# Recurrence products regrouped and the scores' positive part moved to ScalarE, in a hybrid attention and RWKV-7 step

## The chip, the core and the metric

The kernel runs on one core of a Trainium2 chip. The metric is the device time of one execution in microseconds. TensorE does the matrix products, VectorE, ScalarE and GpSimd the elementwise work, and SyncE issues nearly all transfers. Each engine works through its own queue in order.

## The reference

One layer over 2048 prompt tokens and 8 x 8 sample tokens, with a model width of 1024. A combined projection feeds two groups of eight heads of 64: stick-breaking attention, and an RWKV-7 recurrence with a matrix state per head. Both outputs are gated and concatenated, projected back, added to the input and normalised.

```python
# attention: z are the scaled scores plus a bias per head
log_keep = where(mask, log_sigmoid(-z), 0.0)
between = cumsum(log_keep, reverse=True) - log_keep
a = where(mask, exp(log_sigmoid(z) + between), 0.0)
out = einsum('bhqk,bkhd->bqhd', a, v)

# recurrence, per head, for every token
sa = einsum('bhvk,bhk->bhv', S, a_t)
S = S * w_t + sa[..., None] * b_t + v_t[..., None] * k_t
y = einsum('bhvk,bhk->bhv', S, r_t)
```

## The kernel before

The program is planned as a list of operations, each with an engine, a cost, the data it reads and writes, and a priority. `Plan.issue` walks this list like a simulator of its own and emits the operations in the order in which they would start; so the costs, the limits on PSUM banks per kind (`LIMITS`), the latency put on a transfer and the priorities set the order of every engine's queue. All instructions pass through one wrapper and carry line 63 in the profile; they are told apart by the names of their tiles.

The prompt is cut in four slabs of 512 tokens (`hf`), and each slab's head columns in four groups of 128 (`j`), that is two heads. Per slab the projections (`project`, tiles `xh`, `xl`, `wp`; each float32 product is made of three reduced ones) have the lowest priority on TensorE and fill what the rest leaves. `attend(t, j)` handles 512 queries of two heads against all key blocks. Per 128 queries and head it makes a block: scores of 512 keys into a bank (`kt`, `qt`), `softmax_chain`, transposes of the result (`ident`, `T`), an Exp, and the product with the values (`At`, `vt`). In `softmax_chain` ScalarE takes |z + bias| into T, then Exp and Ln in place, VectorE takes max(z + bias, 0) into D, then a backward scan over T and D, and the last step subtracts. The score bank (kind `ZB`, two of them) is held until that last step.

`rw_unit(hf, j)` handles the recurrence of one slab and column group, in 8 chunks of 64 tokens. `rw_pairs` makes the products of keys and queries within a chunk, two heads of 64 rows each (`un.BK`, `un.AR`): for each half of the chunks first the four of head 0 into a bank of kind `EB`, then the four of head 1 into another, then a masked copy into `un.L`. `inverse_a` and `inverse_b` invert the triangular part, with a loop of 31 steps on VectorE. `seq` then does one chunk at a time, and its products on TensorE are called in this text by the names of the functions in the code:

- `fx` (rows named `VV,L`): `un.L` against the stacked state and values, head by head onto the two halves of the partitions
- `fu` (`XT,NN`): the inverse applied to the copy XT of that, one product per head, each into a bank of its own
- `fs` (`VV,BKT`): the new state, both heads on the lower half of the partitions, in different columns
- `fy` (`L,VV`, `AR,VV`, `RS,VV`): the output, two products of 128 rows and two of 64 rows

GpSimd prepares the decayed old state `sw`, and VectorE adds it to the result of `fs` and writes the next state. At the end, sample attention and the output projection (`woh`, `wol`, `orw`) share TensorE with the last attention blocks.

Of the kernel before, what the change touches and what calls it, by code (L numbers as in the profile page):

```python
# [9 lines left out]
F32 = mybir.dt.float32  # L10
# [69 lines left out]
class Plan:  # L80
# [90 lines left out]
    def issue(self, tables):  # L171
# [51 lines left out]
        while done < len(ops):  # L223
            best = None
            for e in engines:
                s, got = pick(e, free[e])
                if s < INF and (best is None or s < best[0]):
                    best = (s, e, got)
            s, e, got = best
            if got is None:  # L230
                got = pick(e, s)[1]
                if got is None:
                    continue
            avail[e].remove(got)
# [36 lines left out]
            done += 1  # L271
            free[e] = s + cost
            busy[e] += cost
            end = s + cost
            if o.lat:
                dma_free = max(dma_free, end + 650.0) + o.lat
                end = dma_free + 1200.0
            for j in outs[i]:
                lag = 0.0 if o.lat else self.LAG.get((e, ops[j].eng), 0.0 if ops[j].eng == e else 170.0)
                ready[j] = max(ready[j], end + lag)  # L280
                left[j] -= 1
                if not left[j]:
                    heapq.heappush(waiting[ops[j].eng], (ready[j], j))
# [59 lines left out]
class Kern:  # L343
# [522 lines left out]
    def rwkv_tiles(self, S):  # L866
# [4 lines left out]
        for i in range(2):  # L871
            u = Unit()
            u.id = i
            u.AR = S.tile([128, 8, 128], F32, "AR").t
            u.BK = S.tile([128, 8, 128], F32, "BK").t
            u.L = [S.tile([128, 8, 128], F32, f"L{h}").t for h in range(2)]
            u.NN = S.tile([128, 8, 64], F32, "NN").t
            nc.gpsimd.memset(u.NN, 0.0)
            u.RS = S.tile([64, 8, 64], F32, "RS").t
            u.WC = S.tile([64, 2, 8], F32, "WC").t  # L880
            self.units.append(u)

# [11 lines left out]
        self.XT = S.ring(2, [128, 64], F32, "XT")  # L894
        self.xts = S.tile([128, 64], F32, "xts")
        self.SW = S.ring(2, [64, 2, 64], F32, "SW")
# [54 lines left out]
    def rw_elem(self, hf, j, t0, N, c0, un):  # L951
# [52 lines left out]
        if smp:  # L1004
            self.copy(self.wc8.t, W3[:, :, 8], r=w3k, w=[self.wc8.k])
        else:
            for h in range(2):
                self.copy(un.WC[:, h, :], W3[self.HR[h], :, 64], r=w3k, w=[("WC", U, i) for i in range(8)])

        self.act(rn, zk, AF.Square, r=kk_, w=[rnk], scale=self.vec("k_k", j))  # L1010
        b3 = self.sums("EB", rn, rnk, self.scratch(hf, 0) if "3" in self.BO and not smp else None)
# [41 lines left out]
    def rw_pairs(self, un):  # L1053

        nc, U = self.nc, un.id
        for c4 in range(0, 8, 4):
            for h in range(2):
                bk = self.bank("EB")
                hr = self.HR[h]
                for i in range(4):  # L1060
                    def f(c=c4 + i, i=i, bk=bk, hr=hr):
                        self.mm(bk.t[:, 128 * i:128 * i + 128], un.BK[hr, c, :], un.AR[hr, c, :], True, True)
                    self.pe(222, f, r=[("AR", U, c4 + i), ("BK", U, c4 + i)], w=[bk.k], mode="C")
                self.tt(un.L[h][:, c4:c4 + 4, :], bk.t.rearrange("p (c x) -> p c x", x=128),
                        self.mask.rearrange("p (o x) -> p o x", o=1).to_broadcast([128, 4, 128]), ALU.mult,
                        r=[bk.k], w=[("L", U, h, c4 + i) for i in range(4)])
# [40 lines left out]
    def inverse_b(self, un):  # L1107
# [27 lines left out]
        self.dma(un.RS, un.AR[64:128, :, 64:128], r=ark, w=[("RS", U)], nbytes=131072)  # L1135

    def seq(self, hf, j, c, un):
        nc, U = self.nc, un.id
# [21 lines left out]
                self.act(VV[lo, 0, 0], self.SP[:, j], AF.Copy, r=[("SP", j)], w=[ks])  # L1160
        lks = [("L", U, 0, c), ("L", U, 1, c)]
        nks = [("NN", U, h, b) for h in range(2) for b in range(2)]
        sw = self.SW.next()
        wc = un.WC[:, :, c:c + 1]
        self.pool(450, lambda: nc.gpsimd.tensor_tensor(out=sw.t, in0=VV[lo, s_, 0], in1=wc.to_broadcast([64, 2, 64]), op=ALU.mult), r=[ks, ("WC", U, c)], w=[sw.k])
# [5 lines left out]
        xt = self.XT.next()  # L1171
        self.copy(xt.t, bx.t[:, 0:64], r=[bx.k], w=[xt.k], prio=-0.5)
        bu = [self.bank("XB"), self.bank("XB")]
        for h in range(2):
            def fu(h=h):
                self.mm(bu[h].t[lo, 0:64], un.NN[hr[h], c, :], xt.t[hr[h], :], True, True)
            self.pe(107, fu, r=nks + [xt.k], w=[bu[h].k], prio=-0.5, mode="B")
        self.copy(VV[lo, s_, 1, 0, :], bu[0].t[lo, 0:64], r=[bu[0].k], w=[ku + (0,)], prio=-0.5)
        self.act(VV[lo, s_, 1, 1, :], bu[1].t[lo, 0:64], AF.Copy, r=[bu[1].k], w=[ku + (1,)], ps=True, prio=-0.5)
        kus = [ku + (0,), ku + (1,)]  # L1180
        bs = self.bank("XB")
        def fs():
# [12 lines left out]
        def fy():  # L1195
            for h in range(2):
                self.mm(yb.t[hr[h], y0:y0 + 64], VV[:, s_, 1, h, :], un.L[h][:, c, 64:128], True, False)
            for h in range(2):
                rt = un.RS[:, c, :] if h else un.AR[lo, c, 64:128]
                self.mm(yb.t[hr[h], y0:y0 + 64], VV[lo, s_, 0, h, :], rt, False, True)  # L1200
        self.pe(500, fy, r=kus + [kv, ks, ("AR", U, c), ("RS", U)] + lks, w=[yb.k], mode="A")
# [363 lines left out]
    def softmax_chain(self, zb, n, bias, bk, car, first, last, rings):  # L1565
# [275 lines left out]
```

## Time and profile before

| | |
|---|---|
| median of three runs | 2165.12 us (2162.68 to 2172.65) |
| profiled execution | 2174.32 us, its span 2172.6 us |
| mean granted TensorE clock | 0.965 of full speed |
| busy: TensorE, weight loads, VectorE, ScalarE, GpSimd | 2068.2, 1570.7, 1764.3, 1322.7, 252.9 us |
| transfers | 380.88 MB, 175 GB/s on average |

The page gives busy time and the chain of waits for the whole span. A float32 product appears as two records, and matmul records overlap: one's end is modelled and lies past the start of the next, so starts are compared and not durations.

### The profile page before, as it was taken

What the parts mean: (1) busy time and instruction counts of PE and PEld (TensorE: products, weight loads), DVE (VectorE), ACT (ScalarE), POOL (GpSimd) and SP (SyncE); (2) the same over time, 40 slices, a digit from 0 to 9 for tenths busy, and PEclk for the clock granted to TensorE, in tenths of its full rate; (3) what the DMA queues carried; (4) which work ended last, traced back from release to release, by engine and by line L of the source; (5) the groups of instructions that cost most, each with busy time, mean ns of one, the idle gap of its engine ahead of it and who ended that gap; (6) DMA issues with size and microseconds to landing.
All of it is one profiled execution on the core that took longest, in us unless ns stands there. A gap on an engine that the chain in (4) does not pass through costs nothing.

```text
span 2172.6 us, 43597 instructions
## 1 busy us (share of the span) xinstructions
PE 2068.2 (95%) x15386; PEld 1570.7 (72%) x15386; DVE 1764.3 (81%) x4085; ACT 1322.7 (61%) x2655; POOL 252.9 (12%) x594
## 2 busy tenths in 40 slices
PE   6799999979999999999999999999999899999998
PEld 6687887757776777777767777877776676767665
DVE  7797687664888889989899898898889798988842
ACT  6544453554655758677567486566468686867731
POOL 4221211100000201010011011011010100000000
PEclk9999989989999999999999999999999799999999
DMA  7975644637666385755634843755744757575654
GB/s 240 328 256 165 200 151 143 197 118 215 180 183 188 101 254 133 216 148 158 187 93 138 241 108 112 209 137 137 203 142 127 207 163 211 161 196 155 192 175 146
DMA packets 346551, 380.88 MB, mean 175 GB/s; under 512 B 127922, under 2 KB 247272, under 8 KB 346332
## 3 DMA queue, kind: packets, MB, share of 16 engines
q1 hardware_dynamic: 345948, 378.00, 59.8%
q8 instruction: 121, 1.98, 0.4%
q14 instruction: 98, 0.80, 0.1%
q0 software_dynamic: 384, 0.10, 0.0%
HBM read 268.94 MB, written 102.76 MB: 171 GB/s over the span
## 4 chain that ended last, share of the span: by engine, by line
PE 66%; DMA 6%; DVE 4%; ACT 2%; SPq 1%; issue 1%; POOL 0%; DVEq 0%; POOLq 0%; ACTq 0%
PE bank L63 66%; DVE D L63 2%; SPq L63 1%; DMA IMP<-d_im 1%; DMA IA<-d_ia 1%; ACT T L63 1%; DMA wp<-d_w 1%; DVE IMP L63 1%; DMA D<-d_g 1%; DVE T L63 0%; DMA d_o<-D 0%; DMA xs<-d_x 0%; DMA kt<-d_k 0%; DMA ev<-d_x 0%; DVE SPT L63 0%
## 5 line engine op out<-in xcount | busy, mean ns | idle before, releaser
L63 PE MATMUL bank<-xh,wp 128*128 128x512 f32 (+2 forms) x2704 | 798.5, 369 | 9.2 <-ACT wp L63 5.6
L63 PEld LDWEIGHTS bank<-xh,wp 128*128 128x128 f32 x2704 | 485.6, 194 | 83.9 <-ACT wp L63 7.4
L63 PE MATMUL bank<-xl,wp 128*128 128x512 f32 (+2 forms) x1352 | 495.5, 367 | 0.0
L63 ACT ACTIVATE T<-T 128x512 f32<-128x512 f32 (+3 forms) x608 | 340.9, 565 | 11.8
L63 PEld LDWEIGHTS bank<-xl,wp 128*128 128x128 f32 x1352 | 261.9, 194 | 33.4 <-issue 2.9
L63 ACT ACTIVATE At<-bank 128x512 f32<-128x512 f32 (+3 forms) x304 | 161.3, 530 | 197.2 <-PE bank L63 186.9
L63 DVE TENSOR_SCALAR D<-bank,sbb 128x512 f32<-128x512 f32 (+3 forms) x304 | 200.6, 661 | 54.6 <-ACT T L63 46.6
L63 DVE TENSOR_TENSOR_SCAN D<-T,car,D 128x512 f32<-128x512 f32 x180 | 230.9, 1283 | 14.5 <-ACT T L63 12.7
L63 PE MATMUL bank<-kt,qt 128*128 128x512 f32 (+3 forms) x640 | 216.7, 414 | 3.8 <-issue 3.3
L63 ACT ACTIVATE T<-bank,sbb 128x512 f32<-128x512 f32 (+3 forms) x304 | 187.7, 620 | 48.0 <-PE bank L63 36.3
L63 DVE SCALAR_TENSOR_TENSOR T<-bank,sbb,D 128x512 f32<-128x512 f32 (+3 forms) x304 | 200.6, 660 | 2.1 <-PE bank L63 0.4
L63 PE MATMUL bank<-woh,orw 128*128 128x512 f32 (+1 forms) x544 | 188.9, 411 | 3.8 <-ACT woh L63 2.8
L63 PE MATMUL bank<-ident,T 128*128 128x128 f32 (+1 forms) x1156 | 175.3, 275 | 13.1 <-DVE T L63 8.8
L63 DVE TENSOR_TENSOR IMP<-IMP,IA 128x2 f32<-128x2 f32 (+30 forms) x496 | 168.0, 339 | 22.3 <-POOL IA L63 16.3
L63 PEld LDWEIGHTS bank<-ident,T 128*128 128x128 f32 (+1 forms) x1156 | 129.3, 142 | 53.8 <-DVE T L63 16.0
L63 PE MATMUL bank<-At,vt 128*64 128x128 f32 x1992 | 149.0, 288 | 0.1
L63 PEld LDWEIGHTS bank<-At,vt 128*64 128x64 f32 x1992 | 111.9, 141 | 36.6 <-issue 28.7
L63 POOL COPY car<-D 128x1 f32<-128x1 f32 x180 | 48.9, 272 | 690.5 <-DVE D L63 639.1
L63 PEld LDWEIGHTS bank<-woh,orw 128*128 128x128 f32 (+1 forms) x544 | 99.5, 187 | 36.9 <-issue 11.9
L63 DVE TENSOR_REDUCE IMP<-IMP 128x1 f32<-128x2 f32 (+30 forms) x496 | 120.9, 244 | 4.9
L63 PEld LDWEIGHTS bank<-kt,qt 128*128 128x128 f32 x640 | 103.8, 196 | 14.3 <-issue 7.7
L63 POOL TENSOR_TENSOR SW<-VV,WC 64x128 f32<-64x128 f32 x128 | 67.8, 533 | 388.9 <-DVE VV L63 292.4
(325 smaller groups left out, 3449.3 us busy)
## 6 DMA issues: line engine op xcount, KB each, us to landing
wp<-d_w SPq DMA_DIRECT2D x198, 512.0 KB
d_w<-wp SPq DMA_DIRECT2D x66, 512.0 KB
kt<-d_k SPq DMA_DIRECT2D x80, 256.0 KB
wraw<-in_w_in SPq DMA_DIRECT2D x66, 256.0 KB
qt<-d_q SPq DMA_DIRECT2D x128, 128.0 KB
orw<-d_o SPq DMA_DIRECT2D x64, 256.0 KB
vt<-out_v_prompt SPq DMA_DIRECT2D x38, 256.0 KB
IA<-d_ia SPq DMA_DIRECT2D x64, 128.0 KB
```

The source lines that it names most:

```text
L63: return f(*[x.real() if isinstance(x, Lz) else x for x in a], **{k: x.real() if isinstance(x, Lz) else x for k, x in kw.items()})
```

## The change

There are six edits. (1) `rw_pairs` takes two banks at once and issues the products of head 0 and head 1 in turn; the plan is told half the cost for each. The limit of `EB` banks goes from 2 to 3. (2) `fu` is one product: XT has a column block per head with zeros in the other head's rows, so one 128-row product gives both heads side by side. The copy into XT is split, the lower half on VectorE, the upper on ScalarE. (3) `fs` writes head 0 to the lower and head 1 to the upper half of the partitions; `WN` holds the decays on 128 partitions for it, and GpSimd writes `sw` in two halves. (4) `fy` uses 128 rows everywhere: head 0 reads the state from a copy `sz` whose upper half is zero, head 1 multiplies with `RS` whose upper half is zero. (5) In `softmax_chain` the positive part is an activation. (6) The plan assumes that a transfer's data arrive 300 ns later than before.

```diff
-                end = dma_free + 1200.0
+                end = dma_free + 1500.0
...
-    LIMITS = {"PB": 3, "EB": 2, "MB": 1, ...
+    LIMITS = {"PB": 3, "EB": 3, "MB": 1, ...
...
-            for h in range(2):
-                bk = self.bank("EB")
-                hr = self.HR[h]
-                for i in range(4):
+            bks = [self.bank("EB") for _ in range(2)]
+            for i in range(4):
+                for bk, hr in zip(bks, self.HR):
...
-                    self.pe(222, f, r=[("AR", U, c4 + i), ("BK", U, c4 + i)], w=[bk.k], mode="C")
+                    self.pe(112, f, r=[("AR", U, c4 + i), ("BK", U, c4 + i)], w=[bk.k], mode="C", share=1.0)
...
-        sw = self.SW.next()
-        wc = un.WC[:, :, c:c + 1]
-        self.pool(450, lambda: nc.gpsimd.tensor_tensor(out=sw.t, in0=VV[lo, s_, 0], in1=wc.to_broadcast([64, 2, 64]), op=ALU.mult), ...)
+        sw, sz = self.SW.next(), self.SZ.next()
+        for h in range(2):
+            wc = un.WC[:, h, c:c + 1].to_broadcast([64, 64])
+            self.pool(250, lambda h=h, wc=wc: nc.gpsimd.tensor_tensor(out=sw.t[hr[h]], in0=VV[lo, s_, 0, h], in1=wc, op=ALU.mult), ...)
+        self.pool(170, lambda: nc.gpsimd.tensor_copy(sz.t[lo], VV[lo, s_, 0, 0]), r=[ks], w=[sz.k])
...
-        self.copy(xt.t, bx.t[:, 0:64], r=[bx.k], w=[xt.k], prio=-0.5)
-        bu = [self.bank("XB"), self.bank("XB")]
-        for h in range(2):
-            def fu(h=h):
-                self.mm(bu[h].t[lo, 0:64], un.NN[hr[h], c, :], xt.t[hr[h], :], True, True)
-            self.pe(107, fu, r=nks + [xt.k], w=[bu[h].k], prio=-0.5, mode="B")
+        self.copy(xt.t[lo, 0], bx.t[lo, 0:64], r=[bx.k], w=[(xt.k, 0)], prio=-0.5)
+        self.act(xt.t[hi, 1], bx.t[hi, 0:64], AF.Copy, r=[bx.k], w=[(xt.k, 1)], ps=True, prio=-0.5)
+        bu = self.bank("XB")
+        self.pe(224, lambda: self.mm(bu.t[lo, 0:128], un.NN[:, c, :], xt.t.rearrange("p h x -> p (h x)"), True, True), ...)
...
-                self.mm(bs.t[lo, 64 * h:64 * h + 64], BKT[:, s_, h, :], VV[:, s_, 1, h, :], True, True)
-        self.pe(270, fs, ...)
+                self.mm(bs.t[hr[h], 0:64], BKT[:, s_, h, :], VV[:, s_, 1, h, :], True, True)
+        self.pe(215, fs, ...)
...
-                rt = un.RS[:, c, :] if h else un.AR[lo, c, 64:128]
-                self.mm(yb.t[hr[h], y0:y0 + 64], VV[lo, s_, 0, h, :], rt, False, True)
-        self.pe(500, fy, ...)
+                st, rt = (VV[:, s_, 0, 1, :], un.RS[:, c, :]) if h else (sz.t, un.AR[:, c, 64:128])
+                self.mm(yb.t[hr[h], y0:y0 + 64], st, rt, False, True)
+        self.pe(330, fy, ...)
...
-        self.ts(d, z, bias, ALU.add, 0.0, ALU.max, r=[zb.k] + bk, w=[D.k])
+        self.act(d, z, AF.Relu, r=[zb.k] + bk, w=[D.k], bias=bias, ps=True)
```

Three places in the order of the queues show what moves. The first is TensorE at one `rw_pairs` of the second slab (`AR`, `BK` are the pair products, `bor` a sum within heads, `zL` the next unit's decay). Before:

```order
L63 MATMUL bank_4_67<-xh_183,bor_161 128x512
L63 MATMUL bank_1_64<-AR_87,BK_88 128x128 x4
L63 MATMUL bank_4_67<-xl_184,bor_161 128x512
L63 MATMUL bank_6_69<-xh_183,wp_190 128x512
L63 MATMUL bank_6_69<-xl_184,wp_190 128x512
L63 MATMUL bank_5_68<-ident_80,T_141 128x128 x4
L63 MATMUL bank_7_70<-kt_136,qt_138 128x512
L63 MATMUL bank_2_65<-AR_87,BK_88 128x128 x4
L63 MATMUL bank_1_64<-AR_87,BK_88 128x128 x4
```

In the change, at the same place:

```order
L63 MATMUL bank_2_65<-AR_87,BK_88 128x128
L63 MATMUL bank_4_67<-AR_87,BK_88 128x128
L63 MATMUL bank_2_65<-AR_87,BK_88 128x128
L63 MATMUL bank_7_70<-xl_192,bor_169 128x512
L63 MATMUL bank_4_67<-AR_87,BK_88 128x128
L63 MATMUL bank_5_68<-xh_191,wp_198 128x512
L63 MATMUL bank_1_64<-ident_80,T_149 128x128 x4
L63 MATMUL bank_6_69<-AR_87,BK_88 128x128 x4
L63 MATMUL bank_2_65<-AR_87,BK_88 128x128 x4
```

The first set of eight now changes bank at every product; the second set still comes as four and four.

The second place is TensorE at the end of a chunk step, from `fu` to `fy`. Before:

```order
L63 MATMUL bank_4_67<-XT_110,NN_99 64x64
L63 MATMUL bank_8_71<-XT_110,NN_99 64x64
L63 MATMUL bank_2_65<-xh_183,wp_190 128x512 x2
L63 MATMUL bank_2_65<-xl_184,wp_190 128x512
L63 MATMUL bank_7_70<-VV_107,BKT_106 64x64 x2
L63 MATMUL bank_1_64<-L_22_97,VV_107 64x64
L63 MATMUL bank_1_64<-L_23_98,VV_107 64x64
L63 MATMUL bank_1_64<-AR_95,VV_107 64x64
L63 MATMUL bank_1_64<-RS_101,VV_107 64x64
```

In the change the same groups (`fs` and `fy` of one step, and `fu` of the next):

```order
L63 MATMUL bank_8_71<-VV_111,BKT_110 64x64 x2
L63 MATMUL bank_6_69<-L_23_99,VV_111 64x64
L63 MATMUL bank_6_69<-L_24_100,VV_111 64x64
L63 MATMUL bank_6_69<-AR_97,SZ_117 64x64
L63 MATMUL bank_6_69<-RS_103,VV_111 64x64
...
L63 MATMUL bank_4_67<-XT_114,NN_101 64x128
```

`fs` and `fy` still stand together; `fu` is one row, twice as wide.

The third place is ScalarE in the last stage, where attention blocks follow each other. Before:

```order
L63 ACTIVATE T_141<-bank_7_70,sbb_159 128x512
L63 ACTIVATE T_141<-T_141 128x512 x2
L63 ACTIVATE At_145<-bank_4_67 128x512
L63 ACTIVATE T_140<-bank_6_69,sbb_159 128x512
L63 ACTIVATE T_140<-T_140 128x512 x2
```

In the change:

```order
L63 ACTIVATE T_149<-bank_4_67,sbb_167 128x512
L63 ACTIVATE D_151<-bank_4_67,sbb_167 128x512
L63 ACTIVATE T_149<-T_149 128x512 x2
L63 ACTIVATE At_152<-bank_1_64 128x512
L63 ACTIVATE T_148<-bank_6_69,sbb_167 128x512
L63 ACTIVATE D_150<-bank_6_69,sbb_167 128x512
```

The row that writes D stands between the Abs and the Exp of its block.

## Rows read from the trace of the kernel before

**Rows 1.** The page: busy time of the engines, and the chain of waits.
```profile
PE 2068.2 (95%) x15386; PEld 1570.7 (72%) x15386; DVE 1764.3 (81%) x4085; ACT 1322.7 (61%) x2655; POOL 252.9 (12%) x594
...
PE 66%; DMA 6%; DVE 4%; ACT 2%; SPq 1%; issue 1%; POOL 0%; DVEq 0%; POOLq 0%; ACTq 0%
```

**Rows 2.** Waits of TensorE by releaser: us in total, times, longest us.
```profile
PE bank L63 <- DVE L L63: 10.9, 2, 9.1
...
PE bank L63 <- DVE tmpke L63: 0.2, 1, 0.2
```

**Rows 3.** Stages: us, busy of PE, PEld, DVE, ACT, POOL, clock, DMA share, GB/s.
```profile
800.00:1000.00 200.00, 199.15 (x1549) 152.64 (x1548) 181.88 (x393) 151.14 (x297) 22.27 (x63) 1.00 0.61 169
1800.00:2000.00 200.00, 198.69 (x1460) 137.38 (x1460) 168.72 (x260) 143.95 (x280) 13.18 (x43) 1.00 0.65 187
```

**Rows 4.** Stage, instructions that read the score bias alone: busy of DVE, ACT, POOL.
```profile
1800.00:2000.00 200.00, 73.02 (x110) 34.70 (x55) 0.00 (x0) 1.00 0.65 187
```

**Rows 5.** Timeline of TensorE around two chunk steps: start us, us, instruction, count.
```profile
1098.97 0.34 PE L63 MATMUL bank<-VV,L 128*64 128x64 f32 x4
1099.23 0.50 PE L63 MATMUL bank<-xh,wp 128*128 128x512 f32 x1
...
1102.09 0.39 PE L63 MATMUL bank<-VV,BKT 128*64 128x64 f32 x3
...
1102.85 0.23 PE L63 MATMUL bank<-neg,idb 128*128 128x128 bf16 x1
...
1109.64 0.40 PE L63 MATMUL bank<-xh,wp 128*128 128x512 f32 x1
1109.97 0.33 PE L63 MATMUL bank<-XT,NN 64*64 64x64 f32 x4
1110.23 0.50 PE L63 MATMUL bank<-xh,wp 128*128 128x512 f32 x1
1110.57 0.39 PE L63 MATMUL bank<-xl,wp 128*128 128x512 f32 x1
1110.80 0.40 PE L63 MATMUL bank<-xh,wp 128*128 128x512 f32 x1
```

**Rows 6.** Timeline of TensorE at pair products: two units.
```profile
1037.05 1.16 PE L63 MATMUL bank<-AR,BK 64*128 64x128 f32 x8
1038.14 0.51 PE L63 MATMUL bank<-xh,wp 128*128 128x512 f32 x1
1038.57 1.71 PE L63 MATMUL bank<-AR,BK 64*128 64x128 f32 x16
...
1156.02 0.48 PE L63 MATMUL bank<-AR,BK 64*128 64x128 f32 x2
```

**Rows 7.** Groups of instructions by shape: busy us, mean ns, idle before.
```profile
L63 DVE TENSOR_SCALAR D<-bank,sbb 128x512 f32<-128x512 f32 x210 | 155.7, 743 | 20.3 <-ACT T L63 18.7 <-ACT rs L63 0.5
L63 ACT ACTIVATE T<-bank,sbb 128x512 f32<-128x512 f32 x210 | 143.6, 686 | 28.3 <-PE bank L63 26.2 <-DVE T L63 0.8
L63 POOL TENSOR_TENSOR SW<-VV,WC 64x128 f32<-64x128 f32 x128 | 67.8, 533 | 388.9 <-DVE VV L63 292.4 <-ACT tmpWi L63 56.2 <-DVE IMP L63 22.2
L63 ACT ACTIVATE VV<-bank 64x64 f32<-64x64 f32 x128 | 27.1, 212 | 44.8 <-PE bank L63 39.3 <-DVE tmprn L63 4.6
```

**Rows 8.** Timeline of ScalarE at one block of the last stage.
```profile
1886.33 0.68 ACT L63 ACTIVATE T<-bank,sbb 128x512 f32<-128x512 f32 x1
1887.04 1.29 ACT L63 ACTIVATE T<-T 128x512 f32<-128x512 f32 x2
1889.58 0.60 ACT L63 ACTIVATE At<-bank 128x512 f32<-128x512 f32 x1 [1.25 <-PE bank L63]
```

**Rows 9.** Timeline of VectorE at the same block.
```profile
1887.86 0.75 DVE L63 TENSOR_SCALAR D<-bank,sbb 128x512 f32<-128x512 f32 x1
1888.71 1.28 DVE L63 TENSOR_TENSOR_SCAN D<-T,car,D 128x512 f32<-128x512 f32 x1
1890.50 0.74 DVE L63 SCALAR_TENSOR_TENSOR T<-bank,sbb,D 128x512 f32<-128x512 f32 x1
```

More of the change, by code (lines that the diff above doesn't have):

```diff
@@ L375 @@
     NEV = 3
-    LIMITS = {"PB": 3, "EB": 2, "MB": 1, "SB": 1, "XB": 2, "YB": 1, "X": 2, "ZB": 2, "TB": 1, "OB": 1, "SA": 1, "SB2": 1, "OY": 4, "SM": 1, "YS": 1}
+    LIMITS = {"PB": 3, "EB": 3, "MB": 1, "SB": 1, "XB": 2, "YB": 1, "X": 2, "ZB": 2, "TB": 1, "OB": 1, "SA": 1, "SB2": 1, "OY": 4, "SM": 1, "YS": 1}
     def __init__(self, tc, I, O):
@@ L878, in rwkv_tiles @@
             nc.gpsimd.memset(u.NN, 0.0)
-            u.RS = S.tile([64, 8, 64], F32, "RS").t
+            u.RS = S.tile([128, 8, 64], F32, "RS").t
+            nc.gpsimd.memset(u.RS[64:128], 0.0)
+            u.WN = S.tile([128, 8], F32, "WN").t
             u.WC = S.tile([64, 2, 8], F32, "WC").t
@@ L893, in rwkv_tiles @@
         self.W3 = S.tile([128, 520], F32, "W3")
-        self.XT = S.ring(2, [128, 64], F32, "XT")
+        self.XT = S.tile([128, 2, 64], F32, "XT")
+        nc.vector.memset(self.XT.t, 0.0)
+        self.SZ = S.ring(2, [128, 64], F32, "SZ")
+        for x in self.SZ.slots:
+            nc.gpsimd.memset(x.t[64:128], 0.0)
         self.xts = S.tile([128, 64], F32, "xts")
-        self.SW = S.ring(2, [64, 2, 64], F32, "SW")
+        self.SW = S.ring(2, [128, 64], F32, "SW")
         self.IA = S.tile([128, 32, 32], F32, "IA")
@@ L1008, in rw_elem @@
                 self.copy(un.WC[:, h, :], W3[self.HR[h], :, 64], r=w3k, w=[("WC", U, i) for i in range(8)])
+            self.copy(un.WN, W3[:, :, 64], r=w3k, w=[("WN", U)])
         self.act(rn, zk, AF.Square, r=kk_, w=[rnk], scale=self.vec("k_k", j))
@@ L1056, in rw_pairs @@
         for c4 in range(0, 8, 4):
-            for h in range(2):
-                bk = self.bank("EB")
-                hr = self.HR[h]
-                for i in range(4):
+            bks = [self.bank("EB") for _ in range(2)]
+            for i in range(4):
+                for bk, hr in zip(bks, self.HR):
                     def f(c=c4 + i, i=i, bk=bk, hr=hr):
                         self.mm(bk.t[:, 128 * i:128 * i + 128], un.BK[hr, c, :], un.AR[hr, c, :], True, True)
-                    self.pe(222, f, r=[("AR", U, c4 + i), ("BK", U, c4 + i)], w=[bk.k], mode="C")
+                    self.pe(112, f, r=[("AR", U, c4 + i), ("BK", U, c4 + i)], w=[bk.k], mode="C", share=1.0)
+            for h, bk in enumerate(bks):
                 self.tt(un.L[h][:, c4:c4 + 4, :], bk.t.rearrange("p (c x) -> p c x", x=128),
@@ L1134, in inverse_b @@
             self.dma(un.L[h][0:64, :, 0:64], un.AR[self.HR[h], :, 0:64], r=ark, w=[("L", U, h, c) for c in range(8)], nbytes=131072)
-        self.dma(un.RS, un.AR[64:128, :, 64:128], r=ark, w=[("RS", U)], nbytes=131072)
+        self.dma(un.RS[0:64], un.AR[64:128, :, 64:128], r=ark, w=[("RS", U)], nbytes=131072)
     def seq(self, hf, j, c, un):
@@ L1162, in seq @@
         nks = [("NN", U, h, b) for h in range(2) for b in range(2)]
-        sw = self.SW.next()
-        wc = un.WC[:, :, c:c + 1]
-        self.pool(450, lambda: nc.gpsimd.tensor_tensor(out=sw.t, in0=VV[lo, s_, 0], in1=wc.to_broadcast([64, 2, 64]), op=ALU.mult), r=[ks, ("WC", U, c)], w=[sw.k])
+        sw, sz = self.SW.next(), self.SZ.next()
+        for h in range(2):
+            wc = un.WC[:, h, c:c + 1].to_broadcast([64, 64])
+            self.pool(250, lambda h=h, wc=wc: nc.gpsimd.tensor_tensor(out=sw.t[hr[h]], in0=VV[lo, s_, 0, h], in1=wc, op=ALU.mult), r=[ks, ("WC", U, c)], w=[(sw.k, h)])
+        self.pool(170, lambda: nc.gpsimd.tensor_copy(sz.t[lo], VV[lo, s_, 0, 0]), r=[ks], w=[sz.k])
         bx = self.bank("XB")
@@ L1170, in seq @@
         self.pe(215, fx, r=lks + [ks, kv], w=[bx.k], prio=-0.5, mode="A")
-        xt = self.XT.next()
-        self.copy(xt.t, bx.t[:, 0:64], r=[bx.k], w=[xt.k], prio=-0.5)
-        bu = [self.bank("XB"), self.bank("XB")]
-        for h in range(2):
-            def fu(h=h):
-                self.mm(bu[h].t[lo, 0:64], un.NN[hr[h], c, :], xt.t[hr[h], :], True, True)
-            self.pe(107, fu, r=nks + [xt.k], w=[bu[h].k], prio=-0.5, mode="B")
-        self.copy(VV[lo, s_, 1, 0, :], bu[0].t[lo, 0:64], r=[bu[0].k], w=[ku + (0,)], prio=-0.5)
-        self.act(VV[lo, s_, 1, 1, :], bu[1].t[lo, 0:64], AF.Copy, r=[bu[1].k], w=[ku + (1,)], ps=True, prio=-0.5)
+        xt = self.XT
+        self.copy(xt.t[lo, 0], bx.t[lo, 0:64], r=[bx.k], w=[(xt.k, 0)], prio=-0.5)
+        self.act(xt.t[hi, 1], bx.t[hi, 0:64], AF.Copy, r=[bx.k], w=[(xt.k, 1)], ps=True, prio=-0.5)
+        bu = self.bank("XB")
+        self.pe(224, lambda: self.mm(bu.t[lo, 0:128], un.NN[:, c, :], xt.t.rearrange("p h x -> p (h x)"), True, True), r=nks + [(xt.k, 0), (xt.k, 1)], w=[bu.k], prio=-0.5, mode="A")
+        self.copy(VV[lo, s_, 1, 0, :], bu.t[lo, 0:64], r=[bu.k], w=[ku + (0,)], prio=-0.5)
+        self.act(VV[lo, s_, 1, 1, :], bu.t[lo, 64:128], AF.Copy, r=[bu.k], w=[ku + (1,)], ps=True, prio=-0.5)
         kus = [ku + (0,), ku + (1,)]
@@ L1183, in fs @@
             for h in range(2):
-                self.mm(bs.t[lo, 64 * h:64 * h + 64], BKT[:, s_, h, :], VV[:, s_, 1, h, :], True, True)
-        self.pe(270, fs, r=[kb, kv] + kus, w=[bs.k], prio=-0.5, mode="A")
+                self.mm(bs.t[hr[h], 0:64], BKT[:, s_, h, :], VV[:, s_, 1, h, :], True, True)
+        self.pe(215, fs, r=[kb, kv] + kus, w=[bs.k], prio=-0.5, mode="A")
         last = c == 7
@@ L1188, in seq @@
             out = self.SP[:, j, h] if last else VV[lo, sn, 0, h, :]
-            self.stt(out, bs.t[lo, 64 * h:64 * h + 64], un.WC[:, h, c:c + 1], sw.t[:, h], ALU.mult, ALU.add,
-                     r=[bs.k, sw.k, ("WC", U, c)], w=[("SP", j)] if last else [("VVS", sn)], prio=-0.5)
+            self.stt(out, bs.t[hr[h], 0:64], un.WN[hr[h], c:c + 1], sw.t[hr[h]], ALU.mult, ALU.add,
+                     r=[bs.k, (sw.k, h), ("WN", U)], w=[("SP", j)] if last else [("VVS", sn)], prio=-0.5)
         if c == 0:
@@ L1198, in fy @@
             for h in range(2):
[L1199 to L1201 removed]
+                st, rt = (VV[:, s_, 0, 1, :], un.RS[:, c, :]) if h else (sz.t, un.AR[:, c, 64:128])
+                self.mm(yb.t[hr[h], y0:y0 + 64], st, rt, False, True)
+        self.pe(330, fy, r=kus + [kv, ks, sz.k, ("AR", U, c), ("RS", U)] + lks, w=[yb.k], mode="A")
     def rw_out(self, hf, j, t0, N, c0, un, yb):
```

## Prediction

> **What bounds the kernel now.** I read the page first: TensorE is busy 2068.2 us of a span of 2172.6 (95%), VectorE 81%, ScalarE 61%, GpSimd 12%, and the chain of waits is 66% TensorE, with nothing else above 6% [rows 1]. So TensorE's queue of work is the bound. What the change is worth is what it takes out of that queue, plus or minus what happens to the 104 us in which TensorE stood still. The list of TensorE's waits splits that idle time: 18 of its rows end on VectorE and sum to 58 us (the longest and the shortest are shown) [rows 2]. The stage table has VectorE at 181.9 of 200 us in the stretch from 800 to 1000, where TensorE is at 199.2, and ScalarE at 144 to 151 [rows 3]: ScalarE has room, VectorE nearly none.
>
> What a small product costs is not its duration, since matmuls overlap. It is the distance from its start to the next start, plus what its neighbours lose. Two 512-column products in a row start 0.23 us apart (1110.57 to 1110.80); the one before a small group takes 0.33 (1109.64 to 1109.97), the one after it 0.34 (1110.23 to 1110.57) [rows 5]. Each visit to a small group thus costs 0.21 us on top of the group itself.
>
> **The change, part by part.** There are 16 units of work (4 slabs of 512 tokens by 4 column groups), so 128 chunk steps, and each step has four small groups on TensorE.
>
> (a) *New state and output* (`fs`, `fy`). Today they stand together and take from 1102.09 to 1102.85, 0.76 us for 12 records [rows 5]: the two heads of `fs` write the same half of the columns and run one after the other, and the last four records of `fy` use 64 rows where the ones ahead use 128. In the change every group has its two heads on different column halves, and all use 128 rows. `fx` has that form today: 4 records, both heads at once, 0.26 us (1098.97 to 1099.23). The two halves of `fy` add four more steps. A step of 128 columns costs (1.16 - 0.48)/6 = 0.113 us, by the rows of eight and of two records of such a product [rows 6]; one of 64 columns costs half, 0.057. The sum is 0.26 + 4 x 0.057 = 0.49, and 0.27 x 128 = 34.6 us are saved. The rows of zeros that fill the operands up to 128 cost nothing: the estimate is made from `fx`, which has 128 rows. Bounds: 34.6, and 0 if the pairs did not overlap.
>
> (b) *`fu`* becomes one product of 128 columns instead of two of 64. Today the two run at once when they stand together (x4 at 1109.97, next start 0.26 later) [rows 5]; the order has them together in 110 steps and apart in 18, where I charge each the same 0.26. With the visits that is (110 + 36) x 0.47 = 68.6 us. The new form, two records of 128 columns, is not in the trace. Bounds: 0.26, as if the width cost nothing, and 0.41, a visit of two records with the same moving width (0.48 less the 0.07 by which a group outlasts the next start) [rows 6]. I take 0.41, the row nearest in width: 128 x (0.41 + 0.21) = 79.4. This part **loses** 11 us; at 0.26 it would win 8.
>
> (c) *Pair products* (`rw_pairs`), 256 of them in 32 sets of eight. Eight records of one head take 1.09 us to the next start; sixteen, where both heads stand together, 1.71 in all or 1.64, and not 2.18 [rows 6]. So heads on different row halves already overlap where they meet. A typical unit today is 8, 16 and 8 records in three visits: 3.82 + 0.63 = 4.45 us. With the heads alternating a set should take the 1.09 of one head, 1.30 with its visit. In the new order 18 of 32 sets are mostly alternated; the others still come head by head, because the second bank comes late. Ten units with one alternated set cost 1.30 + 2.60 (two visits of one head each) and save 0.55 each; three with two such sets save 1.85 each; two in between about 1.2 each; one with none loses 0.75. That is 12.7, taken as 13 us. Bounds: 0 (no more overlap than now) and 16 x 1.85 = 30.
>
> (d) *Relu on ScalarE.* It removes the VectorE pass that writes D, 320 of them, 743 ns for 512 columns. ScalarE's own pass of the same shape, bank and bias, the Abs, takes 686 ns [rows 7]. So at most 320 x 0.69 = 220 us go to ScalarE for about as much from VectorE, and none of it is TensorE's. Where it lands: in 1800 to 2000 ScalarE is busy 143.95 us [rows 3] with 55 Abs passes [rows 4]; 55 x 0.69 = 38 more makes 182 of 200. It fits, narrowly. One block shows the path: Exp and Ln ended at 1888.34 [rows 8], but the scan started at 1888.71, after the VectorE pass of 1887.86 to 1888.61 [rows 9]. With Relu ahead of Exp, Ln would end near 1889.0, so the scan is late by 0.3 and not by 0.69. The block holds its score bank from 1886.33 to 1891.24, 4.91 us; with two banks one block per 2.5 us is possible, and 55 in 200 us are one per 3.6. Cost on the path: zero, with that slack as the cover; without cover, 0.345 us a block (rival 4).
>
> On this the Trainium skill speaks against the change: "ScalarE: Activation LUTs", in its rules for kernel authors, sends relu, max and add to VectorE and not to ScalarE, because VectorE can be up to three times faster. The rows of 743 and 686 ns [rows 7] disagree for this operand, a float32 bank. By the page the pass would be dear on its new engine, and the last rival below likelier than I make it; by the rows the exchange is even.
>
> (e) *Copies and queues.* The copy that feeds `fu` is split: VectorE keeps 64 of its 128 rows at the same width, ScalarE gets 128 x 0.21 = 27 us, the price of its 64x64 copy [rows 7]. `fu` then waits for both, and ScalarE's piece may stand behind one 0.69 us pass; a step's chain takes 3.9 us (1098.97 to 1102.85), and 128 x 4.6 = 589 of 2172, so the recurrence is not the bound. GpSimd's weighted copy (533 ns) becomes two, and a third copy is added: each between half of that and all of it, so at most 1.1 us more per step, 137 us on an engine that is 88% idle. The next state waits for it, but has 3.1 us (1098.97 to 1102.09) until its product starts; a carry copy queued behind it is late by at most 0.5. SyncE issues 2128 transfers in both orders; the assumed landing of 1500 instead of 1200 ns only places consumers later. The third bank for pair products comes out of the eight that all share. There are a few more fills at the start. All of this is taken as zero; bounds 10 us either way, the idle time of a stage.
>
> (f) *TensorE's waits.* VectorE loses some 200 of 1764.3 us, 11%; of the 58 us that end on VectorE that is 6. ScalarE's queue gets longer by 240 of 1322.7; I take 3 back for it. Net -3; bounds -58 (all gone) and +20.
>
> Sum: -34.6 + 11 - 13 - 3 = **-40 us**. The profiled execution took 2174.32; 2174.3 - 40 = 2134. That execution lies 9 us above the median of the runs, 2165.12, so against the median the forecast is **2125 us**.
>
> **Rivals.**
> 1. *VectorE was the hidden brake.* For it: 91% busy from 800 to 1000, and 58 us of waits. If half to all of these go, 29 to 58 instead of 6, the sum is -66 to -95 and the time 2070 to 2100. Against it: TensorE's own row is at 99% in those stages [rows 3]. Chance 0.15.
> 2. *The halves overlap no more than they do.* Then (c) is 0 and the sum -27: 2138. Against it: the sixteen records in 1.71 [rows 6]. 0.05.
> 3. *The time comes back as other waits.* A third of the chain is not TensorE, the list scheduler moves every engine's order, and transfers and the inverse's 31 steps on VectorE don't get shorter. If three quarters of the 40 or more return, 2155 to 2165, no change. 0.14.
> 4. *ScalarE becomes the brake in attention* (slower). Relu stands between Abs and Exp in an in-order queue and lengthens the hold on a score bank; where the two banks set the pace each block costs 0.69/2 = 0.345 us. Gain and loss meet at 40/0.345 = 116 of the 320 blocks; slower by over 0.5% (11 us, about what a measurement can tell from no change) needs 148, and 200 blocks give 2125 + 69 = 2194. For it: 182 of 200 us. Against it: the 1.25 us that ScalarE still waits for TensorE at 1889.58 [rows 8]. 0.11.
>
> **How the numbers follow.** The forecast has 0.55, and its own range is 2105 to 2150, from the bounds of (b) and (c). With rivals 1 and 2, faster gets 0.75; no change 0.14; slower 0.11. The range 2082 to 2165 takes in the forecast, rival 2, rival 3 and most of rival 1; it leaves out rival 4 and the low end of rival 1, within 2 in 10.
>
> **What would show it.** `fs` and `fy` together at 0.45 to 0.52 us; an alternated set of 16 records at 1.1; `fu` at 0.26 to 0.41; TensorE busy about 2030; VectorE near 1565, ScalarE near 1560; Relu near 0.69. The forecast is wrong if TensorE's idle time grows by more than 30 us, or if waits on ScalarE's T, D or XT lead TensorE's list.

## The result and the profile after

| | before | after |
|---|---|---|
| median of the runs taken together | 2163.9 us | **2098.03 us** (4 runs, 2093.44 to 2101.62) |
| ratio, 95% interval | 1 | **0.9692** [0.9652, 0.9731] |
| profiled execution (span) | 2174.32 (2172.6) | 2096.49 (2094.8) |

The change made the kernel 66 us faster. The forecast was 40 us (2125). Its own range was 2105 to 2150, and the whole range, with most of the rivals, 2082 to 2165. So it was right in sign and inside the whole range, but 26 us short, and the time lies 7 us below the forecast's own range.

The page after, busy time of the engines, then the granted clock by slices of the span. It answers to [rows 1]:

```profile
PE 1993.0 (95%) x15130; PEld 1497.9 (72%) x15130; DVE 1607.3 (77%) x3770; ACT 1483.3 (71%) x3115; POOL 313.9 (15%) x854
...
PEclk9899999999999999999999999999998999999999
```

TensorE lost 75 us of busy time and its idle time stayed: 2172.6 - 2068.2 = 104 before, 2094.8 - 1993.0 = 102 after. So the time came out of TensorE's queue and not out of its waits; a busy time near 2030 had been forecast. The waits of TensorE by releaser (us in total, times, longest), which answer to [rows 2]:

```profile
PE bank L63 <- DVE L L63: 11.3, 3, 9.2
...
PE bank L63 <- DVE T L63: 8.2, 10, 2.5
...
PE bank L63 <- ACT XT L63: 3.1, 12, 0.5
```

The second line is the score passes' T; the last is the new wait of `fu` for ScalarE's piece of XT: 12 waits in 128 steps. Stages, with the columns of [rows 3]:

```profile
800.00:1000.00 200.00, 197.58 (x1422) 148.69 (x1421) 165.74 (x397) 154.21 (x315) 33.18 (x88) 1.00 0.63 178
...
1800.00:2000.00 200.00, 192.77 (x1436) 134.31 (x1435) 141.70 (x197) 172.14 (x339) 10.05 (x43) 0.99 0.57 171
```

VectorE has 16 us of room more from 800 to 1000. ScalarE stands at 172 of 200 in the last stage, where 182 was expected.

TensorE at one chunk step (columns of [rows 5]):

```profile
1099.93 0.43 PE L63 MATMUL bank<-XT,NN 128*64 128x128 f32 x2
1100.29 0.50 PE L63 MATMUL bank<-xl,wp 128*128 128x512 f32 x1
...
1101.39 0.34 PE L63 MATMUL bank<-VV,BKT 128*64 128x64 f32 x4
1101.56 0.29 PE L63 MATMUL bank<-L,VV 128*64 128x64 f32 x4
1101.67 0.22 PE L63 MATMUL bank<-AR,SZ 128*64 128x64 f32 x1
...
1101.89 0.51 PE L63 MATMUL bank<-kt,qt 128*128 128x512 f32 x1
```

`fu` takes 0.36 to the next start. `fs` and `fy` take 1101.39 to 1101.89, 0.50, where they took 0.76. TensorE at the pair products of one unit:

```profile
962.05 1.16 PE L63 MATMUL bank<-AR,BK 64*128 64x128 f32 x16
963.15 0.50 PE L63 MATMUL bank<-xl,wp 128*128 128x512 f32 x1
...
965.42 1.16 PE L63 MATMUL bank<-AR,BK 64*128 64x128 f32 x8
966.51 0.50 PE L63 MATMUL bank<-xh,wp 128*128 128x512 f32 x1
```

Sixteen alternating records take 1.10, just what eight of one head take two rows below; [rows 6] had them at 1.64 to 1.71.

Groups by shape (columns of [rows 7]), then ScalarE and VectorE at one block, as in [rows 8, 9]:

```profile
L63 ACT ACTIVATE D<-bank,sbb 128x512 f32<-128x512 f32 x210 | 144.9, 691 | 0.3
L63 ACT ACTIVATE T<-bank,sbb 128x512 f32<-128x512 f32 x210 | 144.2, 686 | 12.5 <-PE bank L63 11.4
L63 POOL TENSOR_TENSOR SW<-VV,WC 64x64 f32<-64x64 f32 x256 | 93.1, 366 | 395.2 <-DVE VV L63 358.5 <-DVE IMP L63 26.2 <-DVE WC L63 5.7
```

```profile
1880.56 0.68 ACT L63 ACTIVATE T<-bank,sbb 128x512 f32<-128x512 f32 x1
1881.13 0.69 ACT L63 ACTIVATE D<-bank,sbb 128x512 f32<-128x512 f32 x1
1881.70 1.31 ACT L63 ACTIVATE T<-T 128x512 f32<-128x512 f32 x2
```

```profile
1883.38 1.27 DVE L63 TENSOR_TENSOR_SCAN D<-T,car,D 128x512 f32<-128x512 f32 x1
...
1884.69 0.75 DVE L63 SCALAR_TENSOR_TENSOR T<-bank,sbb,D 128x512 f32<-128x512 f32 x1
```

Relu takes 691 ns (0.69 forecast), but the pass after it starts 0.57 later, since passes in a row overlap: 1880.56, 1881.13, 1881.70. That is why ScalarE's busy time came to 1483 and not to 1560. VectorE gave up less for the same reason: 1607, not 1565. The block holds its score bank from 1880.56 to 1885.44, 4.88 us against 4.91 before.

One line of the profile was not in the forecast at all, the granted clock. The mean over the core, before and then after:

```profile
core 0: 2172.6 us, clock 0.965
```

```profile
core 0: 2094.8 us, clock 0.986
```

The clock has two levels here, 2.4 and 1.2 GHz, so a mean of 0.965 is 7% of the span at 1.2 GHz (152 us), and 0.986 is 2.8% (59 us). Half of the difference lies between 100 and 500 us. Windows of before, and the same of after (columns of [rows 3]):

```profile
100.00:300.00 200.00, 189.71 (x1654) 161.57 (x1654) 156.23 (x516) 94.11 (x227) 39.28 (x62) 0.92 0.63 193
300.00:500.00 200.00, 181.50 (x1484) 147.88 (x1483) 143.74 (x408) 100.10 (x231) 23.64 (x42) 0.91 0.54 163
```

```profile
100.00:300.00 200.00, 188.57 (x1701) 162.79 (x1701) 164.14 (x553) 102.05 (x255) 49.70 (x95) 0.98 0.67 209
300.00:500.00 200.00, 190.57 (x1534) 149.47 (x1533) 141.87 (x386) 120.11 (x293) 28.61 (x79) 0.98 0.65 193
```

### The profile page after: what moved, and what is told of

Read it like the earlier page. It is cut to its first block, busy times and chain, and to the rows that moved or that the text cites. A ratio compares the mean times of both kernels' runs of the same rounds, so it can differ in the third digit from the quotient of the medians.

```text
span 2094.8 us, 43112 instructions
## 1 busy us (share of the span) xinstructions
PE 1993.0 (95%) x15130; PEld 1497.9 (72%) x15130; DVE 1607.3 (77%) x3770; ACT 1483.3 (71%) x3115; POOL 313.9 (15%) x854
## 5 line engine op out<-in xcount | busy, mean ns | idle before, releaser
L63 PE MATMUL bank<-xh,wp 128*128 128x512 f32 (+2 forms) x2704 | 785.5, 364 | 10.6 <-ACT wp L63 5.8
L63 PEld LDWEIGHTS bank<-xh,wp 128*128 128x128 f32 x2704 | 476.7, 190 | 88.4 <-issue 17.5
L63 ACT ACTIVATE T<-T 128x512 f32<-128x512 f32 (+3 forms) x608 | 345.6, 569 | 6.0
L63 PEld LDWEIGHTS bank<-xl,wp 128*128 128x128 f32 x1352 | 257.4, 190 | 37.2 <-issue 8.1
L63 ACT ACTIVATE D<-bank,sbb 128x512 f32<-128x512 f32 (+3 forms) x304 | 189.4, 624 | 14.7 <-DVE T L63 10.2
L63 PE MATMUL bank<-woh,orw 128*128 128x512 f32 (+1 forms) x544 | 184.2, 406 | 8.7 <-DMA orw<-d_o 8.6
L63 PEld LDWEIGHTS bank<-ident,T 128*128 128x128 f32 (+1 forms) x1156 | 124.8, 141 | 55.3 <-DVE T L63 20.3
L63 POOL TENSOR_TENSOR SW<-VV,WC 64x64 f32<-64x64 f32 x256 | 93.1, 366 | 395.2 <-DVE VV L63 358.5
L63 PE MATMUL bank<-At,vt 128*64 128x128 f32 x1992 | 143.9, 281 | 1.6 <-ACT At L63 0.9
L63 DVE TENSOR_TENSOR_SCAN D<-T,D 128x128 f32<-128x128 f32 (+3 forms) x124 | 101.0, 814 | 46.9 <-ACT T L63 40.7
```

The source lines that it names most:

```text
L63: return f(*[x.real() if isinstance(x, Lz) else x for x in a], **{k: x.real() if isinstance(x, Lz) else x for k, x in kw.items()})
```

## The experiments

26 us were to be explained. Three things could have given them: VectorE as a brake that the list of waits doesn't show (rival 1), the clock, or the order that the list scheduler happened to find. All twelve runs, with the mean granted clock (median of each kernel's runs); the last column is explained below the table. The kernel before, run beside each group, had medians from 2160.5 to 2164.1, so times of different rows compare to within some 4 us.

| kernel | median us | ratio, 95% | clock | us at 0.985 |
|---|---|---|---|---|
| before (33 runs beside the others) | 2161.8 | | 0.970 | 2141 |
| after | 2098.0 | 0.9692 [0.9652, 0.9731] | 0.986 | 2099 |
| e1_relu_only | 2137.2 | 0.986 [0.9797, 0.9922] | 0.974 | 2122 |
| e2_no_relu | 2124.6 | 0.9821 [0.9772, 0.987] | 0.980 | 2118 |
| e3_pairs_only | 2160.7 | 0.9992 [0.9958, 1.0026] | 0.964 | 2131 |
| e4_seq_only | 2115.0 | 0.9784 [0.9734, 0.9833] | 0.983 | 2112 |
| f1_relu_on_dve | 2161.4 | 0.9994 [0.9976, 1.0013] | 0.985 | 2161 |
| f2_head_by_head | 2108.9 | 0.9739 [0.9708, 0.977] | 0.982 | 2105 |
| f3_fy_64_rows | 2105.2 | 0.9734 [0.9698, 0.9769] | 0.985 | 2105 |
| g1_no_pairs | 2142.0 | 0.9909 [0.9873, 0.9945] | 0.975 | 2128 |
| g2_no_pairs_1200 | 2108.2 | 0.9754 [0.9697, 0.9812] | 0.988 | 2112 |
| e5_lat_1200 | 2130.7 | 0.9843 [0.9796, 0.9891] | 0.979 | 2122 |
| p1_lat_1400 | 2120.0 | 0.9789 [0.974, 0.9838] | 0.982 | 2115 |
| h1_old_fu | 2096.6 | 0.9703 [0.9648, 0.9758] | 0.981 | 2091 |

**What the clock is worth.** One program doesn't get the same clock in every run. The kernel before had 0.959 to 0.977 over its 33 runs, and 2181 to 2154 us with it. Over 97 runs of the 14 kernels, each taken against its own kernel's mean, 0.01 of granted clock goes with 14.0 us (standard error 1.3). By that slope the last column sets each median to a clock of 0.985. It is a relation among runs, not an edit: that the clock makes the time is read from it, not tried. The Trainium skill, "TensorE: Matmul & The Clock Gate", section Terms, puts the penalty at the throttled time times the part of the clock withheld; by that, 0.01 would be 2% of the span halved, an estimate of some 22 us. The runs show two thirds of it.

### One part alone, planned anew

Each of these kernels was put in order by the scheduler again. e1: before, with the Relu.

```
-        self.ts(d, z, bias, ALU.add, 0.0, ALU.max, ...)
+        self.act(d, z, AF.Relu, ..., bias=bias, ps=True)
```

> The kernel before with Relu on ScalarE and nothing else changed. Work theory (the time follows TensorE's queue, and Relu takes nothing from it): no change, 2155 to 2170. VectorE theory (the 26 us beyond the forecast come from VectorE's relief): 2130 to 2145, granted clock up from 0.965. ScalarE theory (Relu lengthens the hold on the score banks): above 2175.

Measured: 23 us faster, 19 at equal clock, and more than the 3 us that the forecast gave the Relu. The order is new as well; what that alone can do comes below.

e2: after, with that edit reversed.

> The changed kernel with the positive part back on VectorE, replanned. Work theory: same as the changed kernel, 2090 to 2110, clock 0.98 or more. VectorE theory: 2120 to 2135, with VectorE at 81% or more and the clock back near 0.97.

Measured: 26.5 us slower than after, 19 at equal clock, with VectorE at 84% and the clock at 0.980, which is not as low as expected. Both directions agree.

e3: before, with the alternating pair products and their third bank.

```
-    LIMITS = {"PB": 3, "EB": 2, ...
+    LIMITS = {"PB": 3, "EB": 3, ...
...
+            bks = [self.bank("EB") for _ in range(2)]
+            for i in range(4):
+                for bk, hr in zip(bks, self.HR):
```

> The kernel before with the alternated pair products and the third EB bank alone. Work theory: the pair visits fall from 65.9 to some 53 us and from 62 to some 52 visits, the time by 15 to 2145 to 2152, clock as before. Clock theory (half-array products let the clock fall, and fewer of them hold it): 2115 to 2135, clock 0.975 or more.

Measured: no change in time, outside both ranges. By the starts in the timeline the pair products took 58.1 us instead of 65.9, so 8 came out of the queue, and the clock was lower (0.964 against 0.970, 8 us by the slope).

e4: before, with the new `fu`, `fs`, `fy` and their copies.

```
-                self.mm(bs.t[lo, 64 * h:64 * h + 64], BKT[:, s_, h, :], ...)
+                self.mm(bs.t[hr[h], 0:64], BKT[:, s_, h, :], ...)
...
-                self.mm(yb.t[hr[h], y0:y0 + 64], VV[lo, s_, 0, h, :], rt, False, True)
+                self.mm(yb.t[hr[h], y0:y0 + 64], st, rt, False, True)
```

> The kernel before with the new fu, fs and fy and their copies alone. Work theory: fs and fy fall from 0.75 to 0.50 us, fu rises from 0.26 to 0.36, in all 36 us less: 2122 to 2135, clock as before. Clock theory: 2095 to 2115, clock 0.975 or more. Wait theory (the freed time comes back as waits): above 2145.

Measured: 47 us faster than the median of before, 29 at equal clock; the other 18 are the clock, 0.983 with this part alone. So a higher clock goes with the recurrence's new products. The table says the same: the three kernels without the new `fs` and `fy` have 0.964 to 0.974, the eleven with them 0.975 to 0.988. It does not come from them alone: g1 and g2 below, which differ in the order only, have 0.975 and 0.988.

### One part undone in a fixed order

A new plan moves everything. So three kernels keep the queues of after and change one thing. f1 gives the positive part to VectorE, while the planner still counts it as ScalarE's:

```
-        self.act(d, z, AF.Relu, ..., bias=bias, ps=True)
+        self.P.op("ACT", 50 + 0.833 * n + 93, lambda: self.nc.vector.tensor_scalar(out=d, in0=z, scalar1=bias, scalar2=0.0, op0=ALU.add, op1=ALU.max), ...)
```

> The changed kernel with every queue in its order, but each positive part is issued on VectorE at the same place of the plan, so ScalarE is free where Relu stood. VectorE theory (TensorE waits for a VectorE that is late): 2120 to 2145, VectorE busy near 1800, more TensorE idle time and a lower clock. Order theory (Relu gained because the plan came out in a luckier order, not by the engine): 2090 to 2110.

Measured: **63 us slower than after**, more than was expected, and at the same clock where a lower one was expected. TensorE's waits and one stage of this kernel:

```profile
PE bank L63 <- DVE T L63: 26.5, 55, 2.7
...
PE bank L63 <- DVE VV L63: 8.8, 25, 0.8
```

```profile
1000.00:1200.00 200.00, 191.46 (x1517) 138.06 (x1516) 184.33 (x433) 133.67 (x269) 35.30 (x98) 1.00 0.55 156
```

VectorE is at 184 of 200 (176 in the same stretch after), and TensorE waits for T 55 times instead of 10. TensorE's 15130 instructions are issued in the same order, so the starts can be laid side by side. Counted from 0, number 4200 starts at 582.9 us in both; number 9600 at 1302.8 after and 1336.7 here, number 15000 at 2056.5 and 2119.4. The lateness begins there, behind the first 40 or so of the 320 attention blocks, and grows to the end: 63/320 = 0.20 us a block on average. Of the 63, 34 stand in the page as idle time (136 against 102) and 28 as busy time (2021.4 against 1993.0):

```profile
PE 2021.4 (94%) x15130; PEld 1498.0 (69%) x15130; DVE 1783.5 (83%) x4102; ACT 1350.4 (63%) x2783; POOL 311.5 (14%) x854
```

f2 issues the second head's four products after the first's, in the slots in which they alternated:

```
+            prods = [(c4 + i, i, h) for h in range(2) for i in range(4)]
...
+                    def f(bks=bks, prods=prods):
+                        c, x, g = prods.pop(0)
```

> The changed kernel in its own order, but in each set of pair products the four of head 0 are issued first and then the four of head 1, at the same places of the queue. Work theory: a set goes from 1.1 to 1.25 us to 1.64, for 18 sets 8 us, time 2100 to 2110. Null theory (after the single run without effect): 2090 to 2102, though the sets get longer. Clock theory: 2115 or more, clock below 0.98.

Measured: 11 us slower than after. TensorE at the same unit as above:

```profile
974.69 1.71 PE L63 MATMUL bank<-AR,BK 64*128 64x128 f32 x16
976.33 0.50 PE L63 MATMUL bank<-xl,wp 128*128 128x512 f32 x1
```

1.64 again instead of 1.10. All pair products together take 62.1 us and not 52.8, which is 9. At equal clock the kernel is 6 us slower and not 11, so some of the 9 did not reach the end; the two kernels' intervals overlap a little.

f3 reads 64 rows in `fy`'s last two products (four records) instead of 128 with rows of zeros:

```
-                st, rt = (VV[:, s_, 0, 1, :], un.RS[:, c, :]) if h else (sz.t, un.AR[:, c, 64:128])
+                st, rt = (VV[lo, s_, 0, 1, :], un.RS[lo, c, :]) if h else (sz.t[lo], un.AR[lo, c, 64:128])
```

> The changed kernel in its own order, but the last two products of fy read 64 rows again, without the rows of zeros. Work theory: the hole between 128 and 64 rows comes back, 0.15 us in 128 steps, fs and fy at 0.65 us, 19 us in all: 2110 to 2122. Null theory: the step is hidden, 2093 to 2103. If the clock falls as well, above 2125.

Measured: 7 us slower than after, between the two ranges, and the two kernels' intervals overlap. The group in the timeline:

```profile
1096.24 0.34 PE L63 MATMUL bank<-VV,BKT 128*64 128x64 f32 x4
1096.41 0.29 PE L63 MATMUL bank<-L,VV 128*64 128x64 f32 x4
1096.62 0.27 PE L63 MATMUL bank<-AR,SZ 64*64 64x64 f32 x1
...
1096.89 0.50 PE L63 MATMUL bank<-xh,wp 128*128 128x512 f32 x1
```

and the page:

```profile
PE 2011.1 (96%) x15130; PEld 1510.2 (72%) x15130; DVE 1609.3 (77%) x3770; ACT 1483.1 (71%) x3115; POOL 309.4 (15%) x854
```

The group takes 0.65 and not 0.50. The price of going from products of 128 rows to products of 64 is 0.15. In 128 steps that is 19 us, and all of `fs` and `fy` together take 84.7 instead of 66.3 us. Only 7 us reached the end: TensorE's idle time is 2103.4 - 2011.1 = 92.3 us here and 101.8 after, so about half of the price fell into time in which it would have waited.

### How much an order is worth

e5 and p1 do exactly the work of after; only the landing time that the planner assumes for transfers differs:

```
-                end = dma_free + 1500.0
+                end = dma_free + 1200.0
```

> The changed kernel with the assumed landing of transfers back at 1200 ns; the work of every engine is the same, only the order moves. Work theory: 2090 to 2106. Order theory (the order that the plan happens to find is worth tens of microseconds, as the run without the pair products suggests): 2110 to 2145.

> The changed kernel with 1400 instead of 1500 ns, another order of the same work and no reason of its own to be better or worse. Work theory: 2090 to 2106. Order theory: anywhere from 2090 to 2145, and not beside the 1200 and the 1500 in order of size.

Measured: 2130.7 with 1200, 2120.0 with 1400, 2098.0 with 1500. VectorE and ScalarE are as busy as after, within 8 us, in both. So **a new order of equal work moves the time by up to 33 us**, 23 at equal clock; the other ten are the clock that the order gets. The page of e5, and the first line of its waits:

```profile
PE 2016.4 (94%) x15130; PEld 1512.6 (71%) x15130; DVE 1611.4 (75%) x3770; ACT 1480.4 (69%) x3115; POOL 312.8 (15%) x854
```

```profile
PE bank L63 <- DVE T L63: 17.2, 12, 5.0
```

In e5 TensorE waits 17.2 us for VectorE's T, 8.2 after, and its idle time is 2135.3 - 2016.4 = 119 us, where it is 102 after and 104 before.

e5 is at the same time the change without its edit (6). So that edit, which was forecast as nothing, is worth 33 us beside the other five, and without it the kernel lies 6 us from the forecast of 2125.

g1 and g2 are after without the pair part, planned with 1500 and with 1200:

```
-    LIMITS = {"PB": 3, "EB": 3, ...
+    LIMITS = {"PB": 3, "EB": 2, ...
...
-            bks = [self.bank("EB") for _ in range(2)]
-            for i in range(4):
-                for bk, hr in zip(bks, self.HR):
+            for h in range(2):
+                bk = self.bank("EB")
+                hr = self.HR[h]
+                for i in range(4):
```

> The changed kernel with the pair products and the two EB banks of before, replanned. Work theory: 15 us more, 2108 to 2118. Null theory (as in the run of the pairs alone): 2085 to 2102, then the pair products give nothing in either surrounding.

> The new recurrence products and Relu, with the pair products, EB banks and landing time of before: the two parts that paid alone (0.9784 and 0.986). If they add and the pair products give 11 us as in the fixed order: 2095 to 2115. If the pair products are needed, as in the run without them: 2130 to 2150.

Measured: 44 us slower than after, which is outside both ranges, and 10. One part can't be worth both. Beside e5, which has the pairs and the same 1200, g2 is even 23 faster (11 at equal clock). Only f2, 11 us or 6 at equal clock, says what the pairs do, and in one order. The two runs also show edit (6) the other way round: without the pairs, 1500 is 34 us slower than 1200. A later assumed landing is thus no gain in itself; that it gave a good order in the change is luck.

h1 takes the one part back that was forecast to lose: `fu` as two products of 64 columns, and the copy into XT undivided, with the two XT buffers of before.

```
-        bu = self.bank("XB")
-        self.pe(224, lambda: self.mm(bu.t[lo, 0:128], un.NN[:, c, :], xt.t.rearrange("p h x -> p (h x)"), True, True), ...)
+        bu = [self.bank("XB"), self.bank("XB")]
+        for h in range(2):
+            def fu(h=h):
+                self.mm(bu[h].t[lo, 0:64], un.NN[hr[h], c, :], xt.t[hr[h], :], True, True)
```

> The changed kernel with fu as two products of 64 rows and the undivided copy into XT. Work theory: where the two stand together 0.26 instead of 0.36 us, 13 us less at best, 5 to 10 with those that come apart: 2085 to 2098. Theory of the page on drains and of the wide product being free: no change or slower, 2098 to 2115.

Measured: 2096.6 (2086.9 to 2104.5), no different from after, and 8 us faster at equal clock. `fu` is back at 0.26 us and all of them at 39.9 us instead of 45.9; six or eight us are less than an order moves. No kernel tried beat the change.

## Why the prediction was right, and 26 us short

By its own steps; distances from start to next start are medians over each trace.

- **(a) `fs` and `fy`**: 0.49 forecast, 0.499 measured (0.754 before). 0.255 x 128 = 32.6, and 9 visits fewer are 2 more: 34.5 against the forecast's 34.6.
- **(b) `fu`** was mis-sized. The forecast took 0.41, the nearest row in width; measured 0.363 (0.262 before). The row that was taken, of the pair products, has 64 rows and 128 columns, `fu` has 128 and 64. 46.5 - 38.3 = 8.2 dearer (by the sums over each trace, 45.9 and 40.6, it is 5), and 19 visits fewer give 4 back: it loses 4 and not 11.
- **(c) Pair products**: 65.9 to 52.8 us in all (with what of it ran at 1.2 GHz), and ten visits fewer: 15 against 13. An alternated set of sixteen takes 1.10, as the forecast had it. Rival 2 falls.
- **(d) Relu**: 691 ns; the block is no longer than before. Rival 4 needed ScalarE to hold the banks; it stands at 172 of 200 us, and T's and D's waits don't lead TensorE's list. The pass takes 691 ns there against 743 on VectorE, and f1 shows what VectorE's would cost in this order. The Trainium skill's advice to leave relu to VectorE ("ScalarE: Activation LUTs", rules for kernel authors), whose figure of up to about three times is given for bf16, doesn't hold for these float32 rows.
- **(e)** XT's new wait costs TensorE 3.1 us, inside the bounds. The assumed landing of edit (6) was part of the same term and taken as zero, with bounds of 10 us. e5 measures 33 for it, 23 at equal clock: this is the term that was most out.
- **(f) Waits**: VectorE's rows of TensorE's list fell from 58 to 46.5, ScalarE's and the transfers' rose by 4 each: -4 against the forecast's -3. All idle time together went from 104 to 102, so rival 3 falls.

The steps thus give 34.5 - 4 + 15 + 4, about 50, where the forecast had 40. **What it missed is the clock**, which has no term in it: 0.970 to 0.986 in the runs is 22 us by the slope, and 50 + 22 = 72 stands against 66 measured. At equal clock the change is worth 2141 - 2099 = 42 us.

**And it missed the order**, which works through the same quantities: in e5 the idle time is 17 us longer than after and the clock lower. Three orders of the changed kernel's work (1200, 1400 and 1500) are 31, 42 and 64 us faster than before. The forecast of 40 lies among them. Its mechanism is borne out, since TensorE's queue got shorter by what the groups save; that the order which was kept lies 26 us above it is for a good part luck.

Why the clock rises stays open. It is unchanged when the Relu is undone in a fixed order (f1), and it is higher with the recurrence's new products (e4), but an order alone moves it nearly as much (g1, g2). What TensorE did before a low stretch differs. Windows of before, in the first slab:

```profile
268.00:274.50 6.50, 6.50 (x71) 5.23 (x70) 4.64 (x14) 1.88 (x9) 0.96 (x3) 1.00 0.59 177
274.90:292.00 17.10, 17.10 (x112) 13.09 (x110) 9.32 (x38) 4.55 (x13) 2.14 (x6) 0.50 0.31 93
```

TensorE is busy for all of the first 6.5 us, for the most part with pair products and chunk-step groups; then the clock stands at 1.2 GHz for 17.1 us. Windows of after, around its longest low stretch:

```profile
1587.20:1593.70 6.50, 3.47 (x34) 2.44 (x33) 5.19 (x7) 5.84 (x13) 4.97 (x11) 1.00 0.52 161
1593.70:1614.20 20.50, 12.29 (x46) 8.06 (x44) 11.06 (x20) 10.88 (x19) 1.85 (x3) 0.50 0.69 204
```

Here TensorE stood still for almost half of the time before the clock fell, and this is the usual case. Of before's 23 low stretches three, 34 us of 152, begin behind TensorE work with hardly a gap, and after has none of that kind. The other twenty, and all eight of after, begin behind stretches with waits. So the busy ones can be 34 us of the 93 by which the low time got shorter. The rest belongs to stretches with waits, although the idle time in all is the same; how the waits are spread must have changed, and no run shows why. No run changed the kind of products and left all else alone. f3, with half the rows in `fy`, kept its clock.

**Rival 1** gave 2070 to 2100, and the time lies in it, but not by its route: the waits fell by 11 us and not by 29 to 58. Its mechanism is real all the same: in a fixed order VectorE's load is worth 63 us (f1). Where the order may adapt it is 19 at equal clock, twice (e1, e2), which is no more than an order alone moves. That it doesn't stand in TensorE's list of waits before, because an order made for a full VectorE avoids them, is argued; part of it reads as busy time (28 of f1's 63).

**What stays open.** The steps and the clock already make 72, so there is no room for another 19 from the Relu; e1, e3 and e4 together make 58 at equal clock, where the change makes 42. Something gives back 16 to 25, and orders of equal work differ by 23. No run can tell an interplay of the parts from the luck of one order.

## What to carry to other kernels

Cost a small matmul group by the distance to the next start plus its visit, and not by its durations: that hit three groups within 7 us each. Beside it, look at the granted clock of both kernels before a difference is explained; here a third of the gain was clock, by the slope. Where a scheduler sets the order, test a part in the order that stands, because a new order of the same work can move the time by more than the part does; and count a constant of the scheduler, like the landing time here, as a part of the change.

## What was not expected of the hardware

- Eight pair products (sixteen records), four of one head and then four of the other, take 1.64 us and not 2 x 1.09: records on the other row half start beside ones that were issued several records earlier. Strict alternation gives 1.10.
- Rows of zeros cost nothing here (0.499 for `fs` and `fy` with them, 0.644 without in f3), while going from 128 to 64 rows inside a group costs 0.15 us.
- ScalarE's passes in a row overlap: 691 ns each, 0.57 us from start to start.
- The granted clock differs between runs of one program (0.959 to 0.977), and 0.01 of it goes with 14 us of 2160.
